# The S5 input operator from repeated powers in a hybrid encoder layer: operator laid out for the host's b, eigenvalue chain at triple rate, finer opening

## The chip, the cores and the metric

The kernel runs on one core of a Trainium2 chip. Its time is the device time of one execution in microseconds (us). The profiled execution gives the busy times, the waits and the trace.

## What is computed

One encoder layer is applied to two groups of tokens, 256 and 512, with the same weights (width 1024, all fp32). After an RMS norm, one projection feeds three mixers: a bidirectional S5 state space model, differential attention and cross-attention into 256 memory tokens. Their outputs are gated, summed and projected, and a SwiGLU feed-forward block follows. The change touches the S5 mixer, whose core is, per direction:

```python
def s5_direction(u, lam_re, lam_im, log_dt, b_re, b_im, c_re, c_im):
    lam = lax.complex(lam_re, lam_im)              # 64 groups x 64 states
    dt = jnp.exp(log_dt)[:, None]
    lam_bar = jnp.exp(lam * dt)
    b_bar = ((lam_bar - 1.0) / lam)[..., None] * lax.complex(b_re, b_im)
    c = lax.complex(c_re, c_im)
    # per chunk of 128 tokens, u of shape (tokens, 64 groups, 16 channels):
    bu = jnp.einsum('bcgh,gph->bcgp', u, b_bar)
    a_cum, s = lax.associative_scan(_lin_op, (lam_bar, bu), axis=1)
    s = s + a_cum * state[:, None]
    y = jnp.einsum('bcgp,ghp->bcgh', s, c).real
```

u comes from the layer's projection; the two directions' y are added to d * u, and a gelu and a half-GLU follow.

## The kernel before

**Order of the work.** TensorE (PE) runs nearly all the time, on fp32 matmuls split in three (each operand as a rounded high part and a rest; names ending in h, l or hi, lo). The program begins with warm-up matmuls on the identity (`warm`, line 751), while the first weights and memory tokens are loaded; then come the memory's keys (mk), values (mv) and queries (mq), with the memory attention (scores ms, softmax mp on ACT, transposes mpT, values mo) fed in between. Two generators run beside these dense matmuls and are advanced by `Pace.tick` with a weight for each unit of dense work: `mem_attend`, and the S5 parameters, first `S5.params` (the eigenvalue chain: exponentials, sine and cosine of `lam * dt`, powers 0 to 7 of `lam_bar`) and then `S5.pack`. At the first query projection, `("q", 0)`, neither is ticked. Every engine executes its instructions in the order that this program gives.

**Weights.** `WStream` loads them in tiles of 512 KB (`wr`, SP's queue) and splits them on ACT (line 666: wh) and VectorE (DVE, line 672: wl), or for the rest with an accumulating DMA on POOL's queue (line 670).

**Parameters of an operator.** The S5 work has 16 operators; each takes 4 groups of channels, and a "quarter" of pack is 4 operators. `pack` scales the powers into A, multiplies them by the complex factor f into F, and scales the raw b by the power z into B; a quarter's A, F and B are written to DRAM in one DMA on POOL's queue (`par_scr`, 512 KB). `fetch` (SP's queue) loads an operator's slice, beside its C.

**u.** `u_chunk` computes u in channel tiles of 128. The tiles are put in SBUF (`ut`, pool `utp` with two buffers for the first four, `utp2` for the last four), their pad columns cleared by POOL, and flushed to DRAM (`u_scr`, line 298, 396 KB each).

**The S5 stage** (`steps`, from about 273 us) runs beside u's second half and the gate projection gl. For each operator:

- `build` (line 321) makes G from C and A, `build_e` (326) makes E from B and F, both by `_outer` on DVE: a broadcast product of 128x1024 (line 308), two of 128x512 (311), two of 128x512 to combine (314, 317).
- `response`: matmuls psK (line 343), the kernel K, through DRAM (`k_scr`), gives the Toeplitz tile TT.
- `weights` (359): E has its states on the partitions; for the matmul with u, positions and channels must lie there, so PE transposes it in eight 128x128 pieces (psE, line 368), and ACT evacuates them to ET in two copies of 128x512 (369).
- `tables` on ACT, `states`: psI = ET times U (line 418), rotation and two scans on DVE (X, W, S); `outputs`: psY = TT U + G S (lines 455 to 457).

An iteration of `steps` works on operators s - 1 to s + 3 at once. Loads on SP stand in the order in which the code issues them.

Of the kernel before, what the change touches and what calls it, by code (L numbers as in the profile page):

```python
# [8 lines left out]
F32 = mybir.dt.float32  # L9
# [11 lines left out]
NK = 99  # L21
NPAR = 400


class S5:
# [15 lines left out]
    def open_dram(self, ctx):  # L41
        tc = self.tc
        self.dr = ctx.enter_context(tc.tile_pool(name="s5d", bufs=1, space=DRAM))
        self.u_scr = [self.dr.tile([128, 8 * NK], F32, name=f"u_scr{m}") for m in range(8)]
        self.k_scr = [self.dr.tile([128, 240], F32, name=f"k_scr{m}") for m in range(16)]
        self.p_scr = [self.dr.tile([128, 4, NPAR - 144], F32, name=f"par_scr{m}") for m in range(4)]

    def open_work(self, ctx):
        self.pq = ctx.enter_context(self.tc.tile_pool(name="s5q", bufs=1))

    @staticmethod
    def par_views(t):
# [3 lines left out]
        return (B, *(f(o, o + 32) for o in range(128, 256, 32)))  # L56

    def params(self, scratch):
# [134 lines left out]
        tt(q, Lr, p8i, mul)  # L193
        tt(fi, fi, q, sub)
        yield

# [24 lines left out]
        self.lam = zr, zi, fr, fi, pwr, pwi  # L221

    def pack(self, scratch):

        nc, A = self.nc, self.A
        v = nc.vector
# [4 lines left out]

        zr, zi, fr, fi, pwr, pwi = self.lam
        split = lambda a: a.rearrange("p (q g) -> p q g", g=4)
# [10 lines left out]
        for qt in range(4):  # L244
            gs = slice(16 * qt, 16 * qt + 16)
            st = scratch.tile([128, 4, NPAR - 144], F32, name=f"par{qt}", tag="par", bufs=3)
            B, Ar, Ai, Fr, Fi = self.par_views(st)

            def cscale(outr, outi, sr, si, ir, ii, w):
                sh = [128, 4, 4, w]  # L250
                tm = scratch.tile([128, 16 * 16], F32, name=f"csc{qt}{w}", tag="csc")[:, 0 : 16 * w]
                tm = tm.rearrange("p (q g w) -> p q g w", g=4, w=w)
                br_, bi_ = (split(a[:, gs]).unsqueeze(3).to_broadcast(sh) for a in (sr, si))
                tt(outr, ir, br_, mul)
                tt(tm, ii, bi_, mul)
                tt(outr, outr, tm, sub)
                tt(outi, ii, br_, mul)
                tt(tm, ir, bi_, mul)
                tt(outi, outi, tm, add)
# [9 lines left out]
            cscale(B[:, :, 0], B[:, :, 1], zr, zi, raw[:, 0], raw[:, 1], 16)  # L269
            nc.gpsimd.dma_start(self.p_scr[qt], st)  # L270
            if qt < 2:
                load(qt + 2)
            yield

    def fetch(self, qd):

        st = self.st[qd] = {}
        t = self.pq.tile([128, 1, NPAR], F32, name=f"par{qd}", tag="par", bufs=3)
        hv, q = divmod(qd, 4)
        self.nc.sync.dma_start(t[:, 0, 0:144], self.A["s5_cd"][qd])  # L280
        self.nc.sync.dma_start(t[:, 0, 144:], self.p_scr[hv][:, q])
        B, Ar, Ai, Fr, Fi = self.par_views(t[:, :, 144:])
        st["C"] = t[:, 0, 0:128].rearrange("p (g c h) -> p g c h", g=4, c=2)
        st["B"] = B[:, 0].rearrange("p c g h -> p g c h")
        st["A"], st["F"] = (Ar[:, 0], Ai[:, 0]), (Fr[:, 0], Fi[:, 0])
# [14 lines left out]

    def _outer(self, tag, qd, bufs, x, parts, conj):

        nc, pq = self.nc, self.pq
        re, im = parts
        W4, W5 = [128, 4, 8, 16], [128, 4, 8, 2, 16]
        o = pq.tile([128, 2, 4, 8, 16], F32, name=f"{tag}{qd}", tag=tag, bufs=bufs)
        tm = pq.tile([128, 2, 4, 8, 16], F32, name=f"pt{tag}{qd}", tag="ptmp", bufs=1)
        nc.vector.tensor_tensor(out=o.rearrange("p c g j h -> p g j c h"), in0=x.unsqueeze(2).to_broadcast(W5),
                                in1=re.unsqueeze(3).unsqueeze(4).to_broadcast(W5), op=ALU.mult)
        for c in range(2):  # L310
            nc.vector.tensor_tensor(out=tm[:, c], in0=x[:, :, 1 - c].unsqueeze(2).to_broadcast(W4),
                                    in1=im.unsqueeze(3).to_broadcast(W4), op=ALU.mult)
            if c and conj:
                nc.vector.scalar_tensor_tensor(out=o[:, c], in0=o[:, c], scalar=-1.0, in1=tm[:, c], op0=ALU.mult,
                                               op1=ALU.subtract)
            else:
                nc.vector.tensor_tensor(out=o[:, c], in0=o[:, c], in1=tm[:, c],
                                        op=ALU.add if c else ALU.subtract)
        return o

    def build(self, qd):

        st = self.st[qd]
        st["G"] = self._outer("G", qd, 4, st["C"], st["A"], True)

    def build_e(self, qd):

        st = self.st[qd]
        st["E"] = self._outer("E", qd, 1, st["B"], st["F"], False)

    def response(self, qd):
# [25 lines left out]
        st["TT"] = TT  # L357

    def weights(self, qd):

        nc, pq, env = self.nc, self.pq, self.env
        st = self.st[qd]
        E = st["E"]
        ET = pq.tile([128, 2, 4, 128], F32, name=f"ET{qd}", tag="ET", bufs=2)
        for c in range(2):
            ps = env.psb(f"psE{qd}{c}")
            for g in range(4):
                nc.tensor.transpose(ps[:, 128 * g : 128 * g + 128], E[:, c, g], env.ident)
            nc.scalar.activation(ET[:, c].rearrange("p g l -> p (g l)"), ps, AF.Copy)
        st["ET"] = ET  # L370

# [95 lines left out]
    def steps(self, y_scr):  # L467
# [8 lines left out]
        for s in range(-3, n + 1):  # L476
            do(self.fetch, s + 3)
            if s < -2:
                continue
            do(self.response, s + 1)  # L480
            do(self.build_e, s + 1)
# [4 lines left out]
            do(self.outputs, s - 1, y_scr)  # L486
            do(self.weights, s + 1)
            do(self.tables, s + 1)
# [209 lines left out]
def hybrid_block(ctx, tc, A, outs, consts):  # L698
# [50 lines left out]
    warm = env.psa("warm")  # L749
    for _ in range(14):  # L750
        pe.matmul(warm[:, 0:128], env.ident, env.ident, start=True, stop=True)
# [314 lines left out]
    with tc.tile_pool(name="nrm", bufs=1) as pool, tc.tile_pool(name="nrmg", bufs=1) as pg:  # L1066
# [7 lines left out]
        def features(src, n):  # L1074
            def load(j):
                t = pool.tile([128, 2 * TOK], F32, name=uid("ft"), tag="ft", bufs=4)
                t = t[:, 0 : 2 * n].rearrange("p (k t) -> p k t", k=2)
                pin(nc.sync.dma_start(t, src[:, 2 * j : 2 * j + 2]))
                return t
# [88 lines left out]
    tc.keep_in_program_order(nc.sync.dma_start(bg, A["b_gate"][0].rearrange("(m p) -> p m", p=128)))  # L1168
    up = uctx.enter_context(tc.tile_pool(name="utp", bufs=2))

    def u_chunk(c, tick):
        w = W.get()
        for m in range(2):
            ut = s5.u_tile(up, 2 * c + m)
            for sg, (c0, n) in enumerate(SEGS):
# [929 lines left out]
def layouts(a):  # L2105
# [10 lines left out]
    b = np.stack([a[n][0].transpose(0, 2, 1, 3).reshape(128, 4, 16, 16) for n in ("s5_b_re", "s5_b_im")], axis=2)  # L2116
    o["s5_bT"] = b.transpose(1, 0, 2, 3, 4)
    c = np.stack([a[n][0].transpose(0, 3, 1, 2).reshape(128, 16, 4, 16) for n in ("s5_c_re", "s5_c_im")], axis=3)
    dg = np.zeros((4, 32, 16, 16), np.float32)
# [31 lines left out]
```

## Time and profile before

| | |
|---|---|
| median of 3 runs | 1741.95 us (1741.73 to 1742.84) |
| profiled execution | 1741.41 us, span 1739.3 us |
| PE busy | 1713.9 us, 99% of the span |
| DVE, ACT, POOL busy | 1340.6, 935.9, 292.9 us |
| granted clock of PE, mean | 0.996 of full speed |
| DMA | 249.9 MB, 144 GB/s on average |

The span is the time from the first to the last record of the trace, and 2.1 us of the execution lie outside it. An engine's busy time is the sum of its instructions' times without overlap; matmuls are pipelined, so that a busy PE is one that has matmuls under way, and not one at its peak.

### The profile page before, as it was taken

To read this page: it belongs to the slowest core of one execution; us is meant where nothing else is said; L and a number is where in the kernel's file an instruction comes from. 1 tells how busy PE (TensorE), PEld (TensorE's weight loads), DVE (VectorE), ACT (ScalarE), POOL (GpSimd) and SP (SyncE) were. 2 spreads that over 40 slices of the span, in tenths; PEclk is the share of its full clock that TensorE was granted. 3 is DMA by queue.
4 is the path that set the end of the run, shared out by engine and by line. 5 is a ranking of instruction groups with operands and counts; after the bars stand their busy time and mean duration, and the time that the engine had idled before them with its cause. 6 is when DMAs were issued, how large, how long until landed. Compare 5 with 4: busy or idle time off the path is not lost.

```text
span 1739.3 us, 29776 instructions
## 1 busy us (share of the span) xinstructions
PE 1713.9 (99%) x11312; PEld 1581.8 (91%) x11312; DVE 1340.6 (77%) x2454; ACT 935.9 (54%) x1911; POOL 292.9 (17%) x306
## 2 busy tenths in 40 slices
PE   9989999999999999999999999999999999999998
PEld 9979887888888999999988898998889898989897
DVE  6876756899988458898877697793678878787876
ACT  6545634866566347877766564452434444444441
POOL 0000000000000011110211120440113334343430
PEclk9989999999999999999999999999999999999999
DMA  9413356675766536755793455663304547475643
GB/s 323 137 60 110 111 143 155 174 192 150 183 165 166 142 81 129 151 134 133 195 173 107 148 161 170 148 184 129 85 25 127 146 110 176 127 170 133 158 128 109
DMA packets 202478, 249.90 MB, mean 144 GB/s; under 512 B 33712, under 2 KB 155840, under 8 KB 202336
## 3 DMA queue, kind: packets, MB, share of 16 engines
q1 hardware_dynamic: 158800, 155.83, 29.4%
q0 software_dynamic: 32448, 67.01, 20.1%
q10 hardware_dynamic: 11088, 25.18, 4.2%
q8 instruction: 89, 1.46, 0.3%
q14 instruction: 53, 0.43, 0.1%
HBM read 173.51 MB, written 52.17 MB: 130 GB/s over the span
## 4 chain that ended last, share of the span: by engine, by line
PE 80%; issue 13%; DVE 3%; DMA 2%; ACT 2%; POOL 1%; SPq 0%; POOLq 0%; ACTq 0%; DVEq 0%
PE br L832 4%; PE br L833 4%; PE br L831 4%; PE up L831 3%; PE up L832 3%; PE up L833 3%; PE gate L832 3%; PE gate L833 3%; PE gate L831 3%; PE dn L831 3%; PE dn L833 3%; PE dn L832 3%; PE qk L833 3%; PE qk L831 3%; PE qk L832 3%
## 5 line engine op out<-in xcount | busy, mean ns | idle before, releaser
L666 ACT ACTIVATE wh<-wr 128x1024 fp32r<-128x1024 f32 x118 | 134.0, 1137 | 80.1 <-PE gl L832 19.2
L672 DVE TENSOR_TENSOR wl<-wr,wh 128x1024 fp32r<-128x1024 f32 x72 | 96.2, 1336 | 52.5 <-ACT wh L666 50.4
L831 PE MATMUL gl<-Hhi,wh 128*128 128x256 f32 (+1 forms) x384 | 133.1, 347 | 0.0
L833 PE MATMUL gl<-Hhi,wl 128*128 128x256 f32 (+1 forms) x384 | 129.3, 337 | 0.0
L832 PE MATMUL gl<-Hlo,wh 128*128 128x256 f32 (+1 forms) x384 | 129.3, 337 | 0.0
L670 POOL DMA_DIRECT2D wl<-wr x46 | 40.1, 879 | 465.4 <-ACT wl L669 457.6
L831 PE MATMUL qk<-wh,Hhi 128*128 128x256 f32 x384 | 108.0, 281 | 0.0
L832 PE MATMUL qk<-wl,Hhi 128*128 128x256 f32 x384 | 107.9, 281 | 0.0
L833 PE MATMUL qk<-wh,Hlo 128*128 128x256 f32 x384 | 107.7, 280 | 0.0
L591 DVE TENSOR_TENSOR wl_S<-ws,wh_S 128x512 fp32r<-128x512 f32 x91 | 69.3, 781 | 23.1 <-ACT wh_S L586 22.6
L586 ACT ACTIVATE wh_S<-ws 128x512 fp32r<-128x512 f32 x91 | 54.1, 625 | 60.8 <-PE up L832 27.2
L831 PEld LDWEIGHTS gl<-Hhi,wh 128*128 128x128 f32 x384 | 72.2, 188 | 10.2 <-issue 2.2
L833 PEld LDWEIGHTS gl<-Hhi,wl 128*128 128x128 f32 x384 | 72.2, 188 | 9.2 <-issue 0.6
L832 PEld LDWEIGHTS gl<-Hlo,wh 128*128 128x128 f32 x384 | 72.3, 188 | 7.6
L831 PEld LDWEIGHTS qk<-wh,Hhi 128*128 128x128 f32 x384 | 72.1, 188 | 0.9
L833 PEld LDWEIGHTS qk<-wh,Hlo 128*128 128x128 f32 x384 | 72.1, 188 | 0.5
L832 PEld LDWEIGHTS qk<-wl,Hhi 128*128 128x128 f32 x384 | 72.1, 188 | 0.5
L1386 DVE TENSOR_REDUCE nm<-sc 128x1 f32<-128x512 f32 (+1 forms) x96 | 56.7, 597 | 14.3 <-PE sc L1381 13.6
L1388 ACT ACTIVATE p<-sc,nm 128x512 f32<-128x512 f32 (+1 forms) x96 | 59.0, 617 | 11.0 <-DVE nm L1386 10.6
L612 POOL TENSOR_TENSOR ws<-wr,ws 128x512 f32<-128x512 f32 x26 | 40.0, 1539 | 119.5 <-DVE wl_S L591 119.5
L586 ACT ACTIVATE wh_A<-wr 128x512 fp32r<-128x512 f32 x65 | 38.0, 623 | 35.6 <-PE up L832 16.5
L1565 DVE TENSOR_TENSOR fs<-fs,up 128x384 f32<-128x384 f32 x70 | 37.5, 548 | 24.0 <-PE up L833 23.2
(695 smaller groups left out, 6229.9 us busy)
## 6 DMA issues: line engine op xcount, KB each, us to landing
wr<-in_w_in_dram SPq DMA_DIRECT2D x48, 512.0 KB, 4.5
wl<-wr POOLq DMA_DIRECT2D x46, 512.0 KB, 5.6
wr<-in_w_gate_up_dram SPq DMA_DIRECT2D x44, 512.0 KB, 4.2
wr<-in_w_branch_dram SPq DMA_DIRECT2D x24, 512.0 KB, 3.6
wr<-in_w_down_dram SPq DMA_DIRECT2D x22, 512.0 KB, 4.6
wr<-in_w_mem_kv_dram SPq DMA_DIRECT2D x16, 512.0 KB, 4.8
wr<-in_w_in_dram SPq DMA_DIRECT2D x32, 256.0 KB, 4.6
p_scr<-de ACTq DMA_DIRECT2D x27, 256.0 KB, 4.5
```

Source lines behind the costliest of these rows:

```text
L586: self.nc.scalar.activation(f(hi), src, AF.Copy)
L591: self.nc.vector.tensor_tensor(out=f(lo), in0=src, in1=f(hi).bitcast(F32), op=ALU.subtract)
L612: gt(out=s4, in0=A12, in1=s2, op=sub)
L666: self.nc.scalar.activation(hi, r, AF.Copy)
L670: self.nc.gpsimd.dma_start(lo, r.bitcast(F32R), accum_op=ALU.add)
L672: self.sub.tensor_tensor(out=lo, in0=r, in1=hi.bitcast(F32), op=ALU.subtract)
L831: pe.matmul(ps, wh, xh, start=start, stop=False)
L832: pe.matmul(ps, wh, xl, start=False, stop=False)
L833: pe.matmul(ps, wl, xh, start=False, stop=stop)
L1386: v.tensor_reduce(out=nm[:, m : m + 1], in_=ps, axis=AX.X, op=ALU.max, negate=True)
L1388: act.activation(pm[:, 0:n], ps, AF.Exp, bias=nm[:, m : m + 1], accum_out=s1s[:, tt : tt + 1] if m == 0 else s2)
L1565: v.tensor_tensor(out=o, in0=x, in1=y, op=add)
```

## The change

- **Input operator.** `build_e` no longer makes E with states on the partitions. The host lays b out with positions and channels on the partitions, repeated eight times (`s5_bE`, 512 KB for each operator); `pack` makes the powers times z f (`fp`), transposes them on PE (two 128x128 pieces per quarter, fT), copies them to `ft` on ACT and writes them to DRAM repeated over the 16 channels by four DMAs of 512 KB on POOL's queue (`f_scr`). `fetch_e` loads both for an operator, on SP's queue, and `build_e` multiplies them: two DVE products of 128x1024 and two steps of 128x512, in place in b's tile. `weights` goes, with its transposes and copies. `raw` b is still scaled into B, which the kernel K needs.
- **G.** The powers come with signs laid out (`ArS`, `AiN`), and G is four products of 128x512 and one sum of 128x1024.
- **Eigenvalues.** `params` multiplies z f once (six small DVE steps more), and the chain is ticked also at `("q", 0)`, at three times the weight.
- **Opening.** The first weight tile and the first token tile are loaded in two pieces each, alternating, the weight split in two, and there are 11 warm-up matmuls instead of 14.
- **u.** The first four u tiles take buffers of a pool that is used later for keys (`kr`, three buffers) instead of one of their own.

```diff
-NPAR = 400
+NPAR = 368
...
+        self.f_scr = [self.dr.tile([4, 128, 1024], F32, name=f"f_scr{m}") for m in range(4)]
...
+        zfr, zfi = m1r, em1
+        tt(zfr, fr, zr, mul)
+        tt(q, fi, zi, mul)
+        tt(zfr, zfr, q, sub)
+        tt(zfi, fr, zi, mul)
+        tt(q, fi, zr, mul)
+        tt(zfi, zfi, q, add)
...
-            for dst, src in ((Ar, pwr), (Ai, pwi)):
+            for dst, src, sgn in ((Ar, pwr, 1.0), (ArS[:, :, 1], pwr, -1.0), (AiN, pwi, -1.0)):
                 lay = lambda x: x[:, :, gs].rearrange("p m (q g) -> p q g m", g=4)
-                nc.scalar.activation(dst[0:64], lay(src[0:64]), AF.Copy)
-                nc.scalar.activation(dst[64:128], lay(src[64:128, ::-1]), AF.Copy)
+                nc.scalar.activation(dst[0:64], lay(src[0:64]), AF.Copy, scale=sgn)
+                nc.scalar.activation(dst[64:128], lay(src[64:128, ::-1]), AF.Copy, scale=sgn)
             yield
-            cscale(Fr, Fi, fr, fi, Ar, Ai, 8)
+            fp = scratch.tile([128, 2, 128], F32, name=f"fp{qt}", tag="fp")
...
             yield
+            ps = env.psb("fT")
+            for c in range(2):
+                nc.tensor.transpose(ps[:, 128 * c : 128 * c + 128], fp[:, c], env.ident)
+            ft = scratch.tile([128, 256], F32, name=f"ft{qt}", tag="ft")
+            nc.scalar.activation(ft, ps[:, 0:256], AF.Copy)
+            fv = self.f_scr[qt].rearrange("q (j h) (g x) -> (q j) h g x", h=16, g=4)
+            for g in range(4):
+                r = slice(32 * g, 32 * g + 32)
+                nc.gpsimd.dma_start(fv[:, :, g], ft[r].unsqueeze(1).to_broadcast([32, 16, 256]))
...
             nc.gpsimd.dma_start(self.p_scr[qt], st)
...
+    def fetch_e(self, qd):
+        st = self.st[qd]
+        hv, q = divmod(qd, 4)
+        b = self.pq.tile([128, 2, 4, 128], F32, name=f"ET{qd}", tag="ET", bufs=3)
+        F = self.pq.tile([128, 4, 2, 128], F32, name=f"F{qd}", tag="F", bufs=2)
+        self.nc.sync.dma_start(b, self.A["s5_bE"][qd])
+        self.nc.sync.dma_start(F.rearrange("p g c x -> p (g c x)"), self.f_scr[hv][q])
+        st["ET"], st["F"] = b, F
...
-    def u_tile(self, pool, mt):
-        ut = pool.tile([128, 8, NK], F32, name=f"ut{mt}", tag="ut")
+    def u_tile(self, pool, keys, mt):
+        if pool is None:
+            ut = keys.tile([128, 4, 256], F32, name=f"ut{mt}", tag="kr", bufs=3)
+            ut = ut.rearrange("p a b -> p (a b)")[:, 0 : 8 * NK].rearrange("p (j k) -> p j k", k=NK)
+        else:
+            ut = pool.tile([128, 8, NK], F32, name=f"ut{mt}", tag="ut")
...
     def build(self, qd):
-        st["G"] = self._outer("G", qd, 4, st["C"], st["A"], True)
+        W5 = [128, 2, 4, 8, 16]
+        x, (ar, ai) = st["C"], st["A"]
+        o = pq.tile(W5, F32, name=f"G{qd}", tag="G", bufs=4)
+        tm = pq.tile(W5, F32, name=f"ptG{qd}", tag="ptmp", bufs=1)
+        for w, y, a in ((o, x, ar), (tm, x[:, ::-1], ai.unsqueeze(1).to_broadcast([128, 2, 4, 8]))):
+            for c in range(2):
+                nc.vector.tensor_tensor(out=w[:, c], in0=y[:, c].unsqueeze(2).to_broadcast(W5[:1] + W5[2:]),
+                                        in1=a[:, c].unsqueeze(3).to_broadcast(W5[:1] + W5[2:]), op=ALU.mult)
+        nc.vector.tensor_tensor(out=o, in0=o, in1=tm, op=ALU.add)
     def build_e(self, qd):
-        st["E"] = self._outer("E", qd, 1, st["B"], st["F"], False)
+        b, F = st["ET"], st.pop("F")
+        W4 = [128, 2, 4, 128]
+        tm = pq.tile(W4, F32, name=f"ptE{qd}", tag="ptmp", bufs=1)
+        re, im = (F[:, :, c].unsqueeze(1).to_broadcast(W4) for c in range(2))
+        nc.vector.tensor_tensor(out=tm, in0=b[:, ::-1], in1=im, op=ALU.mult)
+        nc.vector.tensor_tensor(out=b, in0=b, in1=re, op=ALU.mult)
+        for c, op in enumerate((ALU.subtract, ALU.add)):
+            nc.vector.tensor_tensor(out=b[:, c], in0=b[:, c], in1=tm[:, c], op=op)
...
-    def weights(self, qd):
-        E = st["E"]
-        ET = pq.tile([128, 2, 4, 128], F32, name=f"ET{qd}", tag="ET", bufs=2)
-        for c in range(2):
-            ps = env.psb(f"psE{qd}{c}")
-            for g in range(4):
-                nc.tensor.transpose(ps[:, 128 * g : 128 * g + 128], E[:, c, g], env.ident)
-            nc.scalar.activation(ET[:, c].rearrange("p g l -> p (g l)"), ps, AF.Copy)
...
             do(self.fetch, s + 3)
             if s < -2:
                 continue
+            do(self.fetch_e, s + 2)
...
-    for _ in range(14):
+    for _ in range(11):
         pe.matmul(warm[:, 0:128], env.ident, env.ident, start=True, stop=True)
...
-        W._dma()
-        fm = [mt(0), mt(1)]
+        w0 = W.praw.tile([128, W.HALF], F32, name="wr0_0", tag="wr")
+        ft0, piece = mt(0, 2)
+        for j in range(2):
+            pin(nc.sync.dma_start(w0[:, 512 * j : 512 * j + 512].rearrange("p (k c) -> p k c", k=2),
+                                  W.src[0][0][0][:, 2 * j : 2 * j + 2]))
+            piece[j]()
+        fm = [ft0, mt(1)]
...
-            if k % 4 == 0:
-                W.ahead(0, 1 + k // 4)
+            if k in (0, 2):
+                sl = slice(256 * k, 256 * k + 512)
+                split_evac(wp[0][:, sl], wp[1][:, sl], w0[:, sl])
+            if k == 4:
+                W.ahead(0, 2)
...
             if (what, h) != ("q", 0):
                 mat.tick(u_)
-                par.tick(u_)
+            par.tick(3 * u_ if (what, h) == ("q", 0) else u_)
...
-    up = uctx.enter_context(tc.tile_pool(name="utp", bufs=2))
+    up = None
```

More of the change, by code (lines that the diff above doesn't have):

```diff
@@ L55, in par_views @@
         B = t[:, :, 0:128].rearrange("p q (g c h) -> p q c g h", g=4, c=2)
-        return (B, *(f(o, o + 32) for o in range(128, 256, 32)))
+        return B, t[:, :, 128:192].rearrange("p q (c g x) -> p q c g x", c=2, g=4), f(192, 224)
     def params(self, scratch):
@@ L246, in pack @@
             st = scratch.tile([128, 4, NPAR - 144], F32, name=f"par{qt}", tag="par", bufs=3)
[L247 to L259, printed above, removed]
@@ L261, in pack @@
-            for dst, src in ((Ar, pwr), (Ai, pwi)):
+            B, ArS, AiN = self.par_views(st)
+            Ar = ArS[:, :, 0]
+            sh = lambda w: [128, 4, 4, w]
+            bc = lambda a, w: split(a[:, gs]).unsqueeze(3).to_broadcast(sh(w))
+            csc = scratch.tile([128, 16 * 16], F32, name=f"csc{qt}", tag="csc")
+            tmp = lambda w: csc[:, 0 : 16 * w].rearrange("p (q g w) -> p q g w", g=4, w=w)
+            for dst, src, sgn in ((Ar, pwr, 1.0), (ArS[:, :, 1], pwr, -1.0), (AiN, pwi, -1.0)):
@@ L298, in u_flush, with build @@
         self.nc.sync.dma_start(self.u_scr[mt].rearrange("(j h) (g k) -> h g j k", j=8, k=NK), ut)
-    def _outer(self, tag, qd, bufs, x, parts, conj):
+    def build(self, qd):
         nc, pq = self.nc, self.pq
[L304 to L309, printed above, removed]
-        for c in range(2):
[L311 to L319, printed above, removed]
```

54 lines of the change are left out of this document (36 added, 18 removed).

## The prediction

> **What bounds the kernel now.** I read the busy times first, then the chain that ended last, then what TensorE (PE) waited for, and then the stages that the change touches.
>
> ```profile
> PE 1713.9 (99%) x11312; PEld 1581.8 (91%) x11312; DVE 1340.6 (77%) x2454; ACT 935.9 (54%) x1911; POOL 292.9 (17%) x306
> PE 80%; issue 13%; DVE 3%; DMA 2%; ACT 2%; POOL 1%; SPq 0%; POOLq 0%; ACTq 0%; DVEq 0%
> ```
>
> PE is busy for 99% of the span and carries the chain. So time goes away only where PE work goes away, where PE stops waiting, or where its clock stops falling; what is freed on ACT or VectorE (DVE) counts only if PE waits for it. PE's waits, as engine, line, releaser, total, times, longest:
>
> ```profile
> PE ms L831 <- ACT mp L1042: 4.1, 2, 2.1
> PE warm L751 <- POOL ident masks.py:199: 2.7, 1, 2.7
> PE psK L343 <- issue: 2.5, 1, 2.5
> PE mpT L1054 <- DVE mp L1044: 2.4, 2, 1.9
> ```
>
> Three of the change's places lie here: the warm-up, the memory attention's softmax (ms, mpT) under the eigenvalue chain, and psK, the first matmul of the S5 stage. Inside that stage PE waits for nothing.
>
> **Removed: the operator's transposes.** Each of the 16 operators turned its E with eight 128x128 transposes (psE), evacuated by two ACT copies.
>
> ```profile
> L368 PE MATMUL psE<-ident,E x128: 272/273/273, 293.6 to 571.7; 128*128 128x128 f32 x128
> L369 ACT ACTIVATE ET<-psE x32: 572/584/608, 294.3 to 572.1; 128x512 f32<-128x512 f32 x32
> 535.89 0.87 PE psE L368 x8
> ```
>
> The 273 ns overlap one another; the chain puts eight at 0.87 us (0.109 us each). PE is full there, so 16 x 0.87 = **-13.9 us**. The 32 ACT copies (18.7 us) lie off the path and count nothing. Added on PE: two transposes per quarter for the powers (fT), 8 x 0.109 = **+0.9**.
>
> **The opening.** Start, duration, engine, line, instruction, idle time before and releaser:
>
> ```profile
> 2.69 5.40 PE L751 MATMUL warm<-ident 128*128 128x128 f32 x28 [2.69 <-POOL ident masks.py:199]
> 5.38 1.06 ACT L666 ACTIVATE wh<-wr 128x1024 fp32r<-128x1024 f32 x1 [2.88 <-DMA wr<-in_w_mem_kv_dram]
> 6.47 1.22 DVE L672 TENSOR_TENSOR wl<-wr,wh 128x1024 fp32r<-128x1024 f32 x1 [5.39 <-ACT wh L666]
> 6.75 2.71 ACT L826 ACTIVATE memThi<-ft,gcols 128x512 fp32r<-128x512 f32 x4 [0.32 <-DMA ft<-in_memT_dram]
> 7.85 0.36 PE L831 MATMUL mk<-wh,memThi 128*128 128x256 f32 x1
> ```
>
> 14 warm-up matmuls show as 28 and end where the first mk starts: (7.85 - 2.69)/28 = 0.184 us each, so three fewer (six shown) free 1.1 us. The first loads are halved and the split that took 1.06 + 1.22 runs on half a tile, so the first mk operands should be there by about 6.5 instead of 7.7. Nothing gains if the smaller transfers land no earlier (0); all that can be gained is the warm-up's 1.1. The split's rows are nearest: **-1.0**.
>
> **Eigenvalues at triple rate.** The chain's steps, which so far were not handed out during the first query projection, now run there at three times their rate; but its first input is a DMA that waits on POOL, and the instruction order on ACT between the two softmaxes still changes function tables.
>
> ```profile
> 73.13 0.58 POOL L90 DMA_DIRECT2D s5lamT<-in_s_lamT_dram  x1 [70.38 <-DVE Hlo L824]
> 104.51 1.28 ACT L1042 ACT_TABLE_LOAD   x1 [1.72 <-DVE mnm L1039]
> 105.80 0.56 ACT L1042 ACTIVATE mp<-ms,mnm,rqy 128x256 f32<-128x256 f32 x1
> 106.36 0.59 ACT L823 ACTIVATE pTh<-mpT 128x512 fp32r<-128x512 f32 x1
> 106.00:108.00 2.00, 1.49 (x7) 1.49 (x8) 1.51 (x8) 1.49 (x5) 0.00 (x0) 0.50 0.00 0
> ```
>
> The order of the engines there stays almost what it was; one thing moves: pTh (0.59) now stands ahead of the table load, so the exponential after it starts later by that much: **+0.6** (from -6, if the waits shrink, to +1.3, one more table load). The six DVE products for the powers are small and lie beside it.
>
> **The start of the S5 stage** is the uncertain term. Before:
>
> ```profile
> 265.90 6.81 DMA u_scr<-ut
> 272.98 0.35 SPq L280 DMA_DIRECT2D par<-in_s_cd_dram  x1
> 276.04 1.23 DVE L308 TENSOR_TENSOR G<-par 128x1024 f32<-128x1024 f32 x1 [8.01 <-DMA par<-in_s_cd_dram]
> 277.19 1.29 DVE L311 TENSOR_TENSOR ptG<-par 128x512 f32<-128x512 f32 x2
> 282.58 1.07 PE L343 MATMUL psK<-G,par 64*32 64x128 f32 x32 [2.54 <-issue]
> ```
>
> PE ended its u matmuls at 282.58 - 2.54 = 280.0 and then waited for G0, which waited for par0, which waited for the fourth u write (265.90) because its buffer came from there. In the new program u's first tiles live elsewhere, so that wait is gone; in its place par0's load waits for all sixteen writes of the powers (f_scr): four 512 KB DMAs on POOL's queue per quarter, from one single-buffered tile ft. Thus ft3 cannot be evacuated before quarter 2's writes land, and behind ft3 on ACT stand u's fifth copy and two weight splits; the copy is waited for by u's fifth write, the splits by matmuls that come after psK on PE. On POOL the memsets of that u tile stand between the writes. Rows for the positions and the prices (DMA rows: count, KB, us to landing; window row: busy of PE, PEld, DVE, ACT, POOL, clock, DMA share, GB/s):
>
> ```profile
> 259.73 0.39 PE L831 MATMUL u<-Hhi,wh 128*128 128x512 f32 x1
> 240.00:242.00 2.00, 2.00 (x19) 2.00 (x18) 1.00 (x5) 2.00 (x3) 0.00 (x0) 1.00 0.78 249
> par_scr<-par POOLq DMA_DIRECT2D x4, 512.0 KB, 3.8
> u_scr<-ut SPq DMA_DIRECT2D x8, 396.0 KB, 6.0
> kst<-kst POOLq DMA_DIRECT2D x16, 192.0 KB, 3.3
> 284.00:286.00 2.00, 2.00 (x11) 2.00 (x11) 2.00 (x4) 0.20 (x2) 0.00 (x0) 0.50 0.17 42
> ```
>
> The third fT pair stands just ahead of the matmul at 259.73. Call T the time of a quarter's four writes. 249 GB/s at a share of 0.78 is 319 at full share: 2.1 MB take 6.6 us, and par_scr's 3.8 us less its own 1.6 leaves 2.2 us of latency: T = 8.8. The u write of 265.90 falls between quarters 2 and 3 and takes 6.0 - 2.2 = 3.8 us, 1.9 per quarter: **T = 10.5**, about. Chain: fT2 and ft2 by 260.8, T, ft3 0.5, T, then par0's issue and landing (3.3, by 272.98 to 276.04) and four steps of about 1.2 us for G0 (4.9; two of 128x512 take 1.29). Sum: 269.5 + 2T. PE gets there near 280.0 + 0.9 + 0.6 - 1.0 = 280.5 (the position of fT2 moved with it only by the last three terms, 0.3). The stall is 2T - 10.8 or so: about 10.3 for T = 10.5, +7.8 over the 2.54. A wait of 2.54 already gave a clock of 0.50 in 284 to 286; a longer one pays that once too, +0.7 for its tail. **+8.5**. Ends: T = 6.5 (nothing shares the queue and the latency hides) gives a stall of 2.2, 0; T = 14 (below) gives 17.2, +15.4. If G0 is there when PE is, the 2.54 and at least the 1.0 lost to the clock in the last row go: -3.5.
>
> The Trainium skill, TensorE: Matmul & The Clock Gate, Part 1: The HAM clock gate, says the clock has two rates only and comes back after some 3.4 us of work; this trace agrees in size, with 0.50 in that window. By it the clock's price is the same after a wait of 2.5 and of 10 us, and the sum would be 0.7 lower.
>
> **Inside the stage.**
>
> ```profile
> L317 DVE TENSOR_TENSOR E<-E,ptE 128x512 f32<-128x512 f32 x28 | 18.1, 687 | 0.2
> L308 DVE TENSOR_TENSOR E<-par 128x1024 f32<-128x1024 f32 x14 | 17.1, 1219 | 0.0
> 300.00:560.00 260.00, 259.71 (x2109) 229.28 (x2107) 237.70 (x293) 175.59 (x394) 18.92 (x22) 1.00 0.66 168
> ```
>
> DVE builds G in as many element steps as before: 1.22 + 2 x 0.69 + 2 x 0.69 against 4 x 0.69 + 1.22. E falls from 1.22 + 4 x 0.69 = 3.96 to two 128x1024 products and two 128x512 steps, 3.8. Each operator adds 1 MB of loads (b and powers, 512 KB each) on SP's queue, ahead of weight loads; the powers' load waits until DVE is through with E of two operators earlier, b's until PE is through with its states of three earlier.
>
> ```profile
> 340.00:400.00 60.00, 60.00 (x478) 53.12 (x478) 57.72 (x74) 38.29 (x87) 3.42 (x4) 1.00 0.68 178
> 400.00:460.00 60.00, 59.86 (x490) 53.41 (x489) 53.61 (x65) 37.42 (x84) 5.17 (x6) 1.00 0.66 162
> 460.00:510.00 50.00, 50.00 (x412) 43.87 (x411) 45.85 (x57) 33.19 (x75) 2.58 (x3) 1.00 0.59 158
> 510.00:525.00 15.00, 14.86 (x118) 12.80 (x117) 14.30 (x16) 8.89 (x26) 0.86 (x1) 1.00 0.82 206
> ```
>
> PE's 60 us of 340 to 400 become 57.2 (by the psE rows an operator takes (571.7 - 293.6)/15 = 18.5 us, now 17.6), and DVE's 57.7 become 57.2: just full. The stretches behind have 10% left. 16 MB more over some 300 us is 56 GB/s, or 0.17 of the engines, onto 0.59 to 0.82: room, but little in the last. I take **+1.0** for waits for DVE and feeds, between 0 and all of the saving, 13.
>
> **Sum against the profiled 1741.4 us:** -13.9 + 0.9 - 1.0 + 0.6 + 8.5 + 1.0 = -3.9, so 1737.5. The median of the runs shown, 1741.95, is 0.5 above the profiled run: **1738.0**. The measurement can tell 0.2%, 3.5 us.
>
> **Rivals.** *The powers arrive in time* (T at 6.5 or less): the +8.5 is 0, and the time is 1729.5. For it: 512 KB alone take 3.8 us. Against: u's write and weight loads share the engines in the same 20 us.
>
> *The powers' writes run at half rate* (slower or no better). Each reads 32 partitions only. The kst row reads 64 partitions: 192 KB take 3.3, less 2.2 of latency 1.1, so 2.9 us per 512 KB against 1.6 for par_scr from 128. Four are 11.7 + 2.2 = 14 = T; the stall is 17.2, the term +15.4, and the time 1745; with u's write on top, 1749. It ends slower once T passes 14. The Trainium skill, SBUF — State Buffer, Door 1: The DMA port swizzle, holds that 32 or 64 partitions reach only half of the ports, 189 to 196 GB/s at 1 MiB; by its figure four writes would be an estimated 10.7 + 2.2 us and the time 1743. No run here shows it for 32 partitions.
>
> *The stage is paced by DVE or by feeds* (slower): as soon as DVE's work plus its waits for b, powers and parameters passes 17.6 us per operator, PE waits for X and for the weights, and the 0.87 comes back. DVE's 237.7 busy us of 300 to 560 are 17.0 for each of the 14 operators in it, now 16.8; 0.8 us of delay each brings it to that point, 0.9 more each, and the 13.9 less the 1.0 counted is lost: 1751. For it: the row of 340 to 400. Against: the chain in the stage was all PE.
>
> *The triple rate does what its name says*: the waits of ms and mpT (6 us) and the slow clock behind them go, another 10 us off: 1728. Against it stands the unchanged order of the engines.
>
> **Chances.** Forecast 0.42 (own range 1733 to 1744), in time 0.16, half rate 0.22, paced 0.15, triple rate 0.05. Faster by over 0.2% (below 1738.5): 0.22 + 0.16 + 0.05 = 0.43. Within: 0.18 of the forecast and 0.08 of half rate, 0.26. Slower: 0.02 + 0.14 + 0.15 = 0.31. The range 1728 to 1750 leaves out the quick half of the two good cases and the worst of the paced one, below 2 in 10.
>
> **What would show it.** Right: no psE rows, PE busy near 1700; a PE wait of about 10 us on psK, par0 issued near 283 behind the last powers' write, and the clock at 0.5 after it; first mk near 6.8; ms and mpT waits as before. Wrong: a psK wait below 3 or above 17; waits of psY, psI or gl for DVE X or weights spread over 330 to 560; ms waits gone.

## The result: 41 us slower, and the profile after

| | median of the runs | ratio to before, 95% interval |
|---|---|---|
| before | 1742.39 us | |
| changed kernel | 1783.32 us (1779.61 to 1786.03) | 1.0233 [1.0212, 1.0254] |

The prediction said 1738.0, and 1728 to 1750. The page of the changed kernel, lines 1 and 4 (busy times, chain), and then what PE waited for:

```profile
PE 1709.0 (96%) x11186; PEld 1575.2 (88%) x11186; DVE 1338.8 (75%) x2445; ACT 924.5 (52%) x1892; POOL 303.1 (17%) x322
PE 72%; DMA 10%; DVE 9%; ACT 4%; issue 3%; SPq 1%; POOL 0%; DVEq 0%; POOLq 0%; ACTq 0%
```

```profile
PE gl L852 <- ACT glt L1254: 17.2, 8, 5.6
PE u L852 <- ACT ft L280: 15.6, 1, 15.6
PE psK L377 <- DVE G L349: 7.0, 1, 7.0
PE mpT L1075 <- DVE mp L1065: 6.3, 3, 4.1
PE ms L852 <- ACT mp L1063: 4.3, 2, 2.7
```

PE has less to do, but it has lost its place as the only carrier of the chain: DMA's share rose from 2 to 10%, DVE's from 3 to 9%. PE's busy time fell by 4.9 us and not by 13: by the clock records of the two traces it is at work under a granted clock of 0.50 for 31.2 us instead of 11.7, mostly behind the new waits, and half of the difference, 9.7 us, is work that takes longer for it. The span less the busy time went from 25.4 to 74.0 us, and the longest ones are not where the prediction had its one stall: gl waits inside the S5 stage, and u waits ahead of psK.

The spans of the profiled executions, cut where a tile's first matmul (for mo and sc its last one) starts, are (us). The names from e1 on are runs of the section on the experiments; qk and sc are the differential attention's projections and scores, which follow the S5 stage.

| kernel | start to mq | mq to u | u to end of mo | mo to gl | gl to qk (S5 stage) | qk to end of sc | rest | span |
|---|---|---|---|---|---|---|---|---|
| before | 65.8 | 149.2 | 44.5 | 45.8 | 298.6 | 359.7 | 775.7 | 1739.3 |
| changed | 67.2 | 153.3 | 50.1 | 68.9 | 303.4 | 364.7 | 775.4 | 1783.0 |
| e3_spread | 66.6 | 153.3 | 45.2 | 56.8 | 303.3 | 364.6 | 775.4 | 1765.2 |
| e1_once | 66.0 | 152.4 | 45.6 | 54.5 | 331.0 | 359.8 | 775.3 | 1784.6 |
| e5_twice | 68.2 | 153.5 | 45.9 | 49.8 | 307.0 | 360.6 | 775.3 | 1760.3 |
| e6_twice_pool | 67.5 | 154.6 | 45.9 | 55.4 | 289.6 | 361.5 | 776.7 | 1751.2 |
| e14_loads_pool | 67.1 | 153.4 | 49.9 | 70.5 | 291.2 | 366.1 | 775.3 | 1773.5 |
| e9_signs | 66.0 | 149.6 | 45.8 | 54.2 | 290.9 | 360.8 | 775.3 | 1742.6 |
| e12_no_transposes | 66.2 | 149.6 | 44.5 | 45.1 | 285.7 | 359.4 | 775.7 | 1726.2 |
| e13_glt2 | 68.4 | 146.8 | 44.3 | 46.9 | 287.4 | 365.6 | 775.4 | 1734.8 |

Nearly all of the 43.7 us of span stands in five places: mo to gl +23.1, u to mo +5.6, qk to sc +5.0, the S5 stage +4.8 where it should have been 13 shorter, and mq to u +4.1. The start gave +1.4.

**Ahead of the stage.** The chain at the worst place, from the timelines of POOL, ACT and DVE (start, duration, engine, line, instruction, idle time before and releaser), the windows (as in the prediction) and the chain of waits:

```profile
245.07 0.76 DVE L238 TENSOR_TENSOR par<-s5b,zr 128x256 f32<-128x256 f32 x2 [8.56 <-DMA s5b<-in_s_bT_dram]
273.26 2.56 POOL L284 DMA_DIRECT2D f_scr<-ft  x4 [15.33 <-ACT ft L280]
290.93 0.38 ACT L280 ACTIVATE ft<-fT 128x256 f32<-128x256 f32 x1 [13.62 <-DMA f_scr<-ft]
295.19 0.29 POOL L329 MEMSET ut<- 128x8 f32 x6 [13.56 <-DMA u_scr<-ut]
296.33 2.56 POOL L284 DMA_DIRECT2D f_scr<-ft  x4 [0.86 <-issue]
...
288.00:290.00 2.00, 0.00 (x0) 0.00 (x0) 0.00 (x0) 0.00 (x0) 0.00 (x0) 0.50 0.93 293
302.00:304.00 2.00, 2.00 (x19) 2.00 (x18) 0.00 (x0) 0.50 (x1) 0.00 (x0) 1.00 0.93 213
...
278.16 16.80 DMA u_scr<-ut
298.20 10.76 DMA f_scr<-ft
```

Quarter 2's writes are issued from 273.26 and have landed when ft3 starts at 290.93: T, the prediction's name for the time of a quarter's four writes, was 17.7 us. In that time PE stands idle and its clock is at 0.50 (288 to 290). Quarter 3's took from 296.33 to 298.20 + 10.76 = 308.96: 12.6 us, with no other transfer beside them (302 to 304: the DMA engines busy for 0.93 of the time, and 213 GB/s). Beside quarter 2's stood mo's writes, a u write and two weight loads. Before quarter 3's POOL had to clear a u tile, for which the u write had to land first, and that took 16.80 us in the same traffic. Already quarter 0's writes did harm: an s5b load behind them came so late that DVE waited 8.56 us, and PE behind it (4.1 us of mpT's 6.3).

**Inside the stage,** waits of DVE, ACT and SP's queue from 300 to 620, and below the dots the same two of the kernel before:

```profile
DVE ptE L360 <- DMA ET<-in_s_bE_dram: 20.2, 5, 7.5
ACT R L412 <- DVE W L455: 68.5, 14, 8.3
SPq L390 <- DMA k_scr<-K: 36.7, 14, 4.7
SPq L317 <- DVE ET L361: 17.6, 6, 5.6
...
ACT R L391 <- DVE W L434: 43.5, 15, 6.1
SPq L356 <- DMA k_scr<-K: 19.8, 15, 2.4
```

Read from line 4 upwards: SP's queue stands still where the Toeplitz loads (390) wait for k_scr and where a powers' load (317) waits for DVE. b's loads behind them come late, so DVE waits 20.2 us for ET; ACT waits for DVE's scans (68.5 us, before 43.5) and stands ahead of the gate's evacuation, and PE waits 17.2 us for that.

### The profile page after: what moved, and what is told of

Its sections match the earlier page's. It is cut to its first block, busy times and chain, and to the rows that moved or that the text cites. A ratio compares the mean times of both kernels' runs of the same rounds, so it can differ in the third digit from the quotient of the medians.

```text
span 1783.0 us, 29572 instructions
## 1 busy us (share of the span) xinstructions
PE 1709.0 (96%) x11186; PEld 1575.2 (88%) x11186; DVE 1338.8 (75%) x2445; ACT 924.5 (52%) x1892; POOL 303.1 (17%) x322
## 4 chain that ended last, share of the span: by engine, by line
PE 72%; DMA 10%; DVE 9%; ACT 4%; issue 3%; SPq 1%; POOL 0%; DVEq 0%; POOLq 0%; ACTq 0%
PE br L854 4%; PE br L853 4%; PE br L852 4%; PE up L852 3%; PE up L853 3%; PE up L854 3%; PE gate L853 3%; PE gate L854 3%; PE gate L852 3%; PE dn L852 3%; PE dn L854 3%; PE dn L853 3%; PE qk L852 3%; PE qk L854 3%; PE qk L853 3%
## 5 line engine op out<-in xcount | busy, mean ns | idle before, releaser
L852 PE MATMUL gl<-Hhi,wh 128*128 128x256 f32 (+1 forms) x384 | 134.5, 350 | 17.4 <-ACT glt L1254 17.2
L612 DVE TENSOR_TENSOR wl_S<-ws,wh_S 128x512 fp32r<-128x512 f32 x91 | 68.2, 770 | 25.6 <-ACT wh_S L607 22.5
L607 ACT ACTIVATE wh_S<-ws 128x512 fp32r<-128x512 f32 x91 | 54.2, 625 | 63.0 <-PE up L853 26.5
L1424 ACT ACTIVATE p<-sc,nm 128x512 f32<-128x512 f32 (+1 forms) x96 | 59.0, 617 | 11.0 <-DVE nm L1422 10.5
L852 PE MATMUL u<-Hhi,wh 128*128 128x512 f32 (+1 forms) x128 | 45.8, 358 | 15.6 <-ACT ft L280 15.6
L412 ACT ACTIVATE R<-s5kmask,s5rho 128x198 f32<-128x198 f32 x64 | 24.5, 451 | 68.5 <-DVE W L455 68.5
```

The lines of the kernel that those rows point to most:

```text
L412: pin(nc.scalar.activation(R[:, :, g], self.kmask.unsqueeze(1).to_broadcast([128, 2, NK]), AF.Copy, scale=self.rho[:, c]))
L607: self.nc.scalar.activation(f(hi), src, AF.Copy)
L612: self.nc.vector.tensor_tensor(out=f(lo), in0=src, in1=f(hi).bitcast(F32), op=ALU.subtract)
L852: pe.matmul(ps, wh, xh, start=start, stop=False)
L1424: act.activation(pm[:, 0:n], ps, AF.Exp, bias=nm[:, m : m + 1], accum_out=s1s[:, tt : tt + 1] if m == 0 else s2)
```

## The experiments

**The transposes alone,** in the kernel before: ET copied from E straight.

```diff
-            for g in range(4):
-                nc.tensor.transpose(ps[:, 128 * g : 128 * g + 128], E[:, c, g], env.ident)
-            nc.scalar.activation(ET[:, c]..., ps, AF.Copy)
+            nc.scalar.activation(ET[:, c]..., E[:, c]..., AF.Copy)
```

> The kernel before without the 128 transposes: ACT copies E to ET straight, so the operator has states on the wrong side and the S5 outputs are wrong; all else is computed. The prediction's term: 13.9 us less, 1728. Rival (DVE at 96% of its time in 340 to 400 us becomes the bound): 8 us less or fewer, 1734 or more, with waits of PE for X.

Measured 1728.96 us beside 1742.12, a ratio of 0.9934 [0.9922, 0.9946]; the S5 stage took 285.7 instead of 298.6. The main term holds (13.9 worked out, 12.9 in the stage), and DVE is no bound: no wait of PE for X is among its longest.

**The volume of the powers' writes.**

```diff
-        self.f_scr = [... self.dr.tile([4, 128, 1024] ...
+        self.f_scr = [... self.dr.tile([4, 8, 1024] ...
-                nc.gpsimd.dma_start(fv[:, :, g], ft[r].unsqueeze(1).to_broadcast([32, 16, 256]))
+                nc.gpsimd.dma_start(fv[:, g], ft[r])
-        self.nc.sync.dma_start(F..., self.f_scr[hv][q])
+        self.nc.sync.dma_start(F..., self.f_scr[hv][q].unsqueeze(1).to_broadcast([8, 16, 1024]))
```

> The powers are written to DRAM once (4 writes of 32 KB a quarter instead of 512 KB) and repeated over the 16 channels by the load F of each operator, whose bytes stay 512 KB. Theory A (the volume of the sixteenfold writes holds the DMA engines, and with it ft3, the s5b loads and the u writes): the wait of u for ft (15.6 us) and of psK for G (7.0) fall below 3 together, mpT's wait falls from 6.3 to near 2.4, and with the slow clock behind them 30 to 35 us go: about 1750. What is left are the 17 us of gl waiting for glt inside the S5 stage. Theory B (the order of the writes, ft's single buffer and the waits on the queue, and not their volume): writes of 32 KB still cost some 2 to 3 us of latency each in the chain, so a wait near 10 us stays before psK, and the time falls to 1765 to 1770.

Measured 1787.81 us, 1.026 [1.0245, 1.0275]: no gain, where theory A had some 1750, and yet theory A was right ahead of the stage. u's wait for ft fell from 15.6 to 3.9 us and psK's for G is gone (below 3 together was expected), with one of 4.1 us for ut in their place; mo to gl fell from 68.9 to 54.5, u to mo from 50.1 to 45.6. All of it was lost again in the stage, 331.0 instead of 303.4. The chain's row of F's first load, and DVE's wait in the stage:

```profile
283.53 9.03 DMA F<-f_scr
...
DVE ptE L360 <- DMA ET<-in_s_bE_dram: 44.0, 9, 10.8
```

So the repeating load is the new trouble. The next run writes each row twice and repeats less on the load; these are its lines in place of those with a plus above:

```diff
+        self.f_scr = [... self.dr.tile([4, 16, 1024] ...
+            fv = self.f_scr[qt].rearrange("q (j h) (g x) -> (q j) h g x", h=2, g=4)
+                nc.gpsimd.dma_start(fv[:, :, g], ft[r].unsqueeze(1).to_broadcast([32, 2, 256]))
+        self.nc.sync.dma_start(F..., self.f_scr[hv][q].unsqueeze(1).to_broadcast([16, 8, 1024]))
```

> As e1_once, but each row of powers is written twice (64 KB a write) and the load F repeats 16 rows eightfold instead of 8 rows sixteenfold. In e1_once the first psK came at 291 us instead of 317, but F's load took about 9 us and the S5 stage from the first gl to the first qk 331 us instead of 303. Theory 1 (a transfer whose outermost size is 8 is spread over fewer DMA engines): F lands in 4 to 6 us again, the stage is back at 303 or less, psK starts near 291, and the time is about 1755. Theory 2 (repeating on the load is slow as such, for the same rows are read over and over): F still takes 8 to 10 us, and the time stays at 1780 or more.

Measured 1763.04 us, 1.0123 [1.0107, 1.0139], where theory 1 had some 1755; the stage took 307.0 where 303 or less was expected, F landed in 6.7 us in the median instead of 4 to 6, and mo to gl took 49.8. A load that repeats 16 rows eightfold costs little more than a plain one (5.2 us in the changed kernel), one that repeats 8 rows sixteenfold cost 24 us more in the stage. The Trainium skill, DMA: Bandwidth & Descriptors, Why a DMA increments its semaphore by 16 and not by 1, says that a transfer runs on the largest number of engines, up to 16, that divides both of its outermost sizes, so 8 here against 16. The traces agree: each of the 16 loads of F raises its semaphore 8 times from the DMA side in e1_once and 16 times in e5_twice. Since the two runs differ in the number of repeats too, they don't show that the 24 us are due to the number of engines alone.

**The partitions that the writes read,** with bytes, rows and order unchanged:

```diff
-            fv = self.f_scr[qt].rearrange("q (j h) (g x) -> (q j) h g x", h=16, g=4)
+            fv = self.f_scr[qt].rearrange("q (a r) (g x) -> (q a) r g x", r=4, g=4)
-                nc.gpsimd.dma_start(fv[:, :, g], ft[r].unsqueeze(1).to_broadcast([32, 16, 256]))
+                src = ft.unsqueeze(1).to_broadcast([128, 4, 256])
+                nc.gpsimd.dma_start(fv[:, :, g], src)
```

> Each of the sixteen writes of the powers reads all 128 partitions of ft, four rows of 1 KB from each, instead of 32 partitions with sixteen; bytes, destination rows, row length, queue and order are the same. The values land in wrong places, so the S5 operator is a wrong one; all else is computed. Half-rate theory (32 partitions reach only half of the ports): the writes land in 4 to 6 us instead of 9.2 in the median, the waits of u for ft and of psK for G fall from 22.6 us together to below 10, and the time falls by 12 to 25 us, to about 1765. Volume theory (2 MB of 1 KB rows a quarter cost this from any partitions): landing stays at 8 to 10 us and the time within 4 us of 1783.

Measured 1767.25 us, 1.0145 [1.0128, 1.0162]: 16 us less, from a change of the source alone. A write now reads four times as many partitions, and each row four times instead of sixteen; the run can't separate these two. (The prediction's kst row, which moves 64 partitions' rows once each, came out as slow per byte, at an estimated 2.9 us for 512 KB; that speaks for the partitions without settling it.) DMA issues of e3_spread (median us from issue to landing), its chain's last powers' write, and PE's two waits:

```profile
f_scr<-ft POOLq DMA_DIRECT2D x16, 512.0 KB, 5.9
...
285.73 6.38 DMA f_scr<-ft
...
PE u L852 <- ACT ft L280: 8.5, 1, 8.5
PE psK L377 <- issue: 4.1, 1, 4.1
```

In the changed kernel these were

```profile
f_scr<-ft POOLq DMA_DIRECT2D x16, 512.0 KB, 9.2
```

and 10.76. The waits fell from 22.6 us together to 12.6, where below 10 was expected. The last quarter's writes run alone in both kernels: there the four land 2.6 us apart in the changed kernel (from 301.05 to 308.96) and 1.6 us apart in e3_spread (from 287.42 to 292.11). The Trainium skill, SBUF — State Buffer, Door 1: The DMA port swizzle, has 32 partitions at 189 GB/s and 128 at 328, measured at 1 MiB; the ratio of landings here, 9.2 to 5.9, agrees with its direction and roughly its size, and that of the distances, 2.6 to 1.6, is closer still. That the four writes of a quarter cover all partitions between them did not help.

**The single buffer of ft.**

```diff
-            ft = scratch.tile([128, 256], F32, name=f"ft{qt}", tag="ft")
+            ft = scratch.tile([128, 256], F32, name=f"ft{qt}", tag="ft", bufs=2)
```

and fp likewise. 

> ft and fp get two buffers, so that ft3 need not wait until quarter 2's writes have landed; the writes are as large as before. Theory B: u's wait for ft (15.6 us) goes and little comes in its place, so 10 to 18 us less: about 1768. Theory A: the last quarter's writes still stand behind quarter 2's on the same engines, so par0 comes hardly earlier, and most of the 15.6 us turns up before psK: 0 to 8 us less than the changed kernel, 1775 to 1783.

Measured 1766.99 us, 1.0149 [1.0117, 1.0182], 16 us less: theory B's number. But what PE waited for, and the chain:

```profile
PE u L852 <- DVE ut L1219: 15.5, 1, 15.5
...
271.73 25.26 DMA u_scr<-ut
```

The wait for ft became one of the same length for a u write that took 25 us among the powers' writes, so the number was met by luck. What went is PE's wait on psK (7.0 us), which the new order puts beside gl (322.2, gl at 326.1), and parts of the waits of mpT (6.3 to 1.9) and of gl for glt (17.2 to 12.0). Neither theory had that; the run separates the two poorly.

**The queue of the loads,** in e5_twice.

```diff
-        self.nc.sync.dma_start(b, self.A["s5_bE"][qd])
-        self.nc.sync.dma_start(F.rearrange(...), ...)
+        self.nc.gpsimd.dma_start(b, self.A["s5_bE"][qd])
+        self.nc.gpsimd.dma_start(F.rearrange(...), ...)
```

> e5_twice with the loads of b (ET) and of the powers (F) issued on POOL's queue instead of SP's. Queue theory (inside the stage the b load stands behind SP instructions that wait, such as the Toeplitz loads waiting for k_scr, and so DVE, ACT behind it and gl wait): DVE's wait for ET (20 us in the changed kernel) and gl's wait for glt (17 us) fall below 5, and the time falls another 12 to 18 us below e5_twice, to about 1740. Rival (the DMA engines are full in the stage, at 0.8 of their time, and the loads are late on any queue): gl's wait stays above 10 us and the time within 5 us of e5_twice.

Measured 1750.93 us, 1.0044 [1.003, 1.0058], 12 us less than e5_twice but not 1740; the stage took 289.6 instead of 307.0. PE's wait for glt is 6.2 us, where below 5 was expected. DVE's wait for ET all but vanished:

```profile
DVE ptE L360 <- DMA ET<-in_s_bE_dram: 0.4, 1, 0.4
```

The same edit on the changed kernel, with its large writes:

> The changed kernel, large writes and all, with the loads of b and powers on POOL's queue. Theory (inside the stage it is SP's order that loses the transposes' gain, and this is apart from the writes): the stage from the first gl to the first qk falls from 303 to about 290 us, the time from 1783 to about 1770, and the stretch ahead of it stays near 69 us. Rival (the gain in e6_twice_pool hung on the small writes): the stage stays above 298 us.

Measured 1770.50 us, 1.0164 [1.0146, 1.0182]; the stage took 291.2, mo to gl 70.5. PE's wait that was 17.2 us in the changed kernel is now

```profile
PE gl L852 <- ACT glt L1254: 8.3, 9, 1.5
```

In the stage DVE waits for ET no more, and ACT for DVE's scans 39.4 us instead of 68.5. So 12.2 us of the stage's loss are the loads' place on SP's queue, apart from the writes; the other 5.5 over e12_no_transposes (285.7) are not.

**ACT's copies.** The changed pack makes 24 sign-laid copies of powers instead of 16. The groups of copies from pwr from 185 to 235 (busy, mean ns) have 16 copies instead of 8; those from pwi are unchanged in number:

```profile
L264 ACT ACTIVATE par<-pwr 64x128 f32<-64x128 f32 x8 | 3.4, 428 | 0.1
L263 ACT ACTIVATE par<-pwr 64x128 f32<-64x128 f32 x8 | 3.4, 425 | 0.3 <-DMA par_scr<-par 0.2
```

```diff
-                nc.scalar.activation(dst[0:64], lay(src[0:64]), AF.Copy, scale=sgn)
+                (as before for sgn > 0, else) nc.gpsimd.tensor_scalar(out=o_, in0=i_, scalar1=sgn, ..., op0=mul)
```

> e6_twice_pool with the negative copies of the powers (16 of the 24 ACT copies of pack, 0.43 us each) made on POOL. Theory (in all kernels with the change the stretch from the first mq to the first u is 3 to 5 us longer than before, because ACT makes 6 copies a quarter instead of 4 ahead of the softmax, and the chain runs through them at 195 to 201 us): that stretch falls from 154.6 to about 151, and the time by 3 us, to about 1748. Rival (the stretch is longer for the fT transposes and the eigenvalue chain's six steps): within 1 us of e6_twice_pool's stretch.

Measured 1746.88 us, 1.004 [1.0024, 1.0055], beside e6_twice_pool's 1.0044 [1.003, 1.0058], so the total doesn't tell the two apart; the stretch from mq to u does, 149.6 instead of 154.6. The run takes sixteen copies off ACT, eight more than the change had added. On the changed kernel:

> The changed kernel with the negative copies of the powers on POOL, and nothing else. Theory: the stretch from the first mq to the first u falls from 153.3 by 3 to 5 us as in e9_signs, the rest stays, so about 1779. Rival (under the large writes the ACT copies are hidden, for the wait turns up before the S5 stage again): within 1.5 us of 1783.

Measured 1780.89 us, 1.0211 [1.0193, 1.0229]: mq to u fell from 153.3 to 148.9, but u to mo took 52.5, so half of it was waited for again. The time is not apart from the changed kernel's.

**The opening alone,** in the kernel before (two pieces, 11 warm-up matmuls):

> The kernel before with the finer opening alone (two pieces of the first weight and token tiles, 11 warm-up matmuls). The prediction's term: 1.0 us less than before, 1742.4. Rival (the trace of the changed kernel shows its first mk at 7.40 instead of 7.85, but at half clock until 8.2 and with 0.65 us of gaps up to 58 us): no gain, within 0.5 us of before, or up to 1.5 us more.

Measured 1742.44 us, 1.0006 [0.9997, 1.0016]. The first mk and the stretch behind it, and below it that stretch in the kernel before:

```profile
6.77 0.36 PE L831 MATMUL mk<-wh,memThi 128*128 128x256 f32 x1
...
8.00:58.00 50.00, 49.33 (x416) 48.74 (x415) 36.88 (x103) 32.13 (x64) 0.00 (x0) 1.00 0.89 316
...
8.00:58.00 50.00, 50.00 (x427) 50.00 (x427) 40.06 (x106) 32.82 (x66) 0.00 (x0) 1.00 0.90 318
```

mk starts 1.08 us sooner, as worked out, and PE loses 0.67 of it at once in a stretch that was full before (50.00 of 50), waiting for the next token tile. Most of the head start is spent on the wait for the data behind it.

**u's buffers alone,** in the kernel before.

> The kernel before with the first four u tiles in the keys' buffers alone, and nothing else of the change. Theory (par0's first load no longer waits for the fourth u write, and nothing else takes that place): the 2.5 us wait before psK and the half clock behind it go, 3 to 4.5 us less than before, about 1739.5. Rival (the three buffers are shared with keys, so u tiles wait for them, or another load is late next): no change, within 1 us, or a few us more.

Measured 1743.57 us, 1.0006 [0.9997, 1.0016]. psK comes at 273.9 instead of 282.6, but gl at 306.0 instead of 305.3, and a wait of 2.9 us stays before psK. The wait for the fourth u write, which the prediction took off, was no gain to be had. (The memory's keys use these three buffers ahead of u, to 213 us in the changed kernel, and not later.)

**The eigenvalue chain at the old rate,** in the changed kernel.

> The eigenvalue chain is ticked as before the change: not at the first query projection, then at the single rate. All else is the changed kernel. Theory of the prediction (the order of the engines hardly depends on it): within 3 us of 1783, and ms and mpT wait as long at 98 to 116 us. Rival (the chain at triple rate stands ahead of the softmax on DVE and ACT): 3 to 8 us faster, 1775 to 1780.

Measured 1784.74 us, 1.0242 [1.0223, 1.0261]; mq to u 152.6. It changes nothing that can be measured here.

**What is left over,** repaired: the powers written from ACT's queue with two buffers,

```diff
-                nc.gpsimd.dma_start(fv[:, :, g], ft[r]...)
+                nc.scalar.dma_start(fv[:, :, g], ft[r]...)
```

> e6_twice_pool with the powers written from ACT's queue instead of POOL's, and two buffers for ft and fp. Theory (with small writes, what is left before the S5 stage is the order: on POOL the last writes stand behind the clearing of a u tile, which waits 7.7 us for a u write): par0 is issued some 8 us earlier, the waits of u (6.4 and 3.3 us) go, and the time falls by 6 to 10 us, to 1741 to 1745. Rival (the u write itself, or its tile's buffer, holds the next u tile on DVE and ACT whatever the queue): within 3 us of 1751.

Measured 1743.09 us, 1.0003 [0.9993, 1.0013]; mo to gl fell from 55.4 to 42.8, of which u to mo gave back 3.5 (49.4). Then with the signs on POOL and the old rate:

> e9_signs and e10_actq together, and the eigenvalue chain ticked as before the change. Theory (the losses add up): 1738 to 1742, level with the kernel before or up to 4 us faster. Rival (each edit moves the order and the next wait takes its place): 1746 or more.

Measured 1739.11 us, 0.9982 [0.9972, 0.9993]; mq to u took 145.8 beside 149.6 in e9_signs, and whether the rate or the queue did that is not shown. And with a second buffer for the gate tiles (`tag=f"glt{sg}", bufs=2`), every engine's order being that of e11_all:

> e11_all with two buffers for the gate tiles glt. In e11_all ACT still waits 30 us for the flush of glt to land, PE 7 us for ACT, and the stage from the first gl to the first qk takes 291.1 us where the kernel without transposes takes 285.7. Theory (the flush, slower under the added loads, holds the one buffer): gl's wait falls below 3 us, the stage to 287, the time by 3 to 5 us, to about 1735. Rival (ACT stands behind DVE's scans all the same): within 1 us of e11_all.

Measured 1735.41 us, 0.996 [0.9946, 0.9974]: faster than both kernels, by 0.4% than the one before. Its interval and e11_all's touch at 0.997, so the buffer's own worth is not settled by the total; the stage took 287.4 instead of 291.1, within 2 us of the one without transposes. PE's wait for glt is still 5.0 us, where 3 was expected at most.

## Why the prediction was wrong, step by step

**The transposes, -13.9:** right; 12.9 in the stage of e12_no_transposes.

**The opening, -1.0:** with the opening alone the 1.08 us at mk were right, the step that they carry through to the end was not; in the changed kernel mk came at 7.40, and the start to mq took 1.4 us longer. A PE that was full in the kernel before shows that data came in time for the later start, no more.

**Eigenvalues at triple rate, +0.6:** within what can be measured.

**The start of the S5 stage, +8.5:** the chain was the right one (fT, ft's buffer, the writes, par0) and its price was wrong twice, so that the stall of about 10.3 us became 15.6 on u and 7.0 on psK. First T: it was taken at 10.5, from a full-share rate of 319 GB/s and from par_scr, which reads 128 partitions, and a share for u's write; it was 17.7 and, with no other transfer beside it, 12.6. The kst row, from 64 partitions, gave 14 and was set aside as a rival with 0.22. Second, "on POOL the memsets of that u tile stand between the writes" stood in the text without a price: the u write they wait for took 16.8 us instead of 6, being in the same traffic. And most of the stall came ahead of where it was looked for: the prediction let PE run on to psK, but the first u matmul after fT3 itself waits for ft3 (15.6 us). By the code, the PSUM banks are laid out anew at that place, and fT must have been read before; no run tried another place. The chain also began later, with ft2 ready at 273.0 and not at 260.8, mostly because PE had by then lost 11.1 us in the stretches before.

**What was left out:** quarter 0's writes in front of an s5b load on POOL (u to mo, +5.6; 45.2 with the partitions spread), and eight more ACT copies on the chain of the softmax (mq to u, +4.1; gone where sixteen copies leave ACT, 149.6 in e9_signs and 148.9 in e15_signs_alone).

**Inside the stage, +1.0:** it was 17.7 (303.4 in the changed kernel, 285.7 without transposes). The step looked at DVE's busy time and at bytes, and found both just sufficient. The queue's order decided most of it: the loads stood on SP behind instructions that waited 36.7 us for k_scr and 17.6 for DVE, and off that queue 12.2 of the 17.7 went (e14_loads_pool). The paced-stage rival had this result and 0.15, for DVE's fullness and for feeds; the feeds were the greater part, and the last 5.5 us are not assigned.

**The rivals as such:** half rate and paced stage were written as alternatives, with chances that add up. Nothing makes them exclude each other, and both happened. Their prices over the forecast, about 7 to 11 and 13, together give some 1758 to 1762; the rest is the second wait on u's write, the s5b load and the copies.

**Open:** 5.0 us from qk to the end of sc, where nothing was changed. PE waits there 2.1 and 1.1 us for mo's reloads before br (0.6 and 0.2 before). It shows in the profiled executions of e3_spread and e13_glt2 too, and not in those of e1_once, e2_ft2 and e5_twice, so it is tied to no part of the change that was tried. In the changed kernel PE's clock falls to 0.50 for 3.4 us near 930 us too, behind those waits, which it does not in the kernel before; why the reloads come late is open.

## What to carry to other kernels

A transfer moved off the compute engines is paid for in order: ask of each new DMA what stands behind it on its queue, what its instruction waits for, and what shares the engines until it lands. In this kernel data was repeated at less cost on the load, with an outermost size of 16, than on the write from 32 partitions. And rivals that can happen together should have their prices added before the range is drawn.

## What the hardware showed beyond that

Writes of equal bytes, rows and order landed in 9.2 us in the median from 32 partitions and in 5.9 from 128, and the kernel's time differed by 16 us for it. A load that repeats 8 rows sixteenfold, and raises its semaphore 8 times, cost the stage 24 us over one that repeats 16 rows eightfold and raises it 16 times.
